# Three of four RNN heads on channel tiles in place, low halves and a channel sum by DMA, and one more conv pair in the second part

## The chip, the cores and the metric

The kernel runs on one core of a Trainium2 chip. The engines named here are PE (matrix products), ACT (functions of one tensor), DVE (elementwise work on two tensors, and scans), POOL (here it issues DMAs that add to their destination) and SP (here it only issues DMAs). The metric is the device time of one execution in microseconds; lower is better. Three runs of the kernel before took 1533.87 to 1534.23 us, median 1534.11 us.

## The reference, cut to what matters

One layer over 1024 positions and 1024 channels: a norm, two parallel branches, a gated sum and a projection, then an MLP and a final norm.

```python
h = rms_norm(x, g_mix)
z = h @ w_in + b_in                       # 7168 columns
va, ga, xb, gb, sa, sb = split(z, (1024, 1024, 1536, 1536, 1024, 1024))

u = va * sigmoid(ga)                      # conv branch
u = causal_depthwise_conv(u, conv_a_w, conv_a_b)      # 31 taps
u = silu(layer_norm(u, ln_g, ln_b))       # mean over the 1024 channels
y_a = u @ w_a_out

v = causal_depthwise_conv(xb, conv_b_w, conv_b_b)     # RNN branch, 4 taps
r = sigmoid(block_diag(v, w_rg_a) + b_rg_a)           # 16 heads of 96 channels
i = sigmoid(block_diag(v, w_rg_x) + b_rg_x)
log_a = -8 * r * softplus(-lam)
a, mult = exp(log_a), sqrt(-expm1(2 * log_a))         # mult is 1 at position 0
v = scan(h[t] = a[t] * h[t-1] + mult[t] * i[t] * v[t])
y_b = (v * gelu(gb)) @ w_b_out

x = x + (sigmoid(sa) * y_a + sigmoid(sb) * y_b) @ w_o
x = x + square(relu(rms_norm(x, g_mlp) @ w_1)) @ w_2
return rms_norm(x, g_final)
```

## The kernel before

Tensors lie with channels on the 128 partitions and the 1024 positions along the free axis. Every fp32 operand of a product is split in a high and a low half, and a product is three matmuls (high by high, low by high, high by low). A low half is made in one of two ways: ACT copies the high half and DVE subtracts it from the source, or `split_dma` lets ACT write a negated high half, ACT write the high half, and a DMA of POOL's queue add the source (L65 to L67).

**The first part.** The loop `for s in range(3, NC1)` runs over column tiles of w_in, 128 columns each; CH lists them and s is called a slot. A column tile is 48 matmuls (`chunk_mm`, L726). In a slot PE does 36 of them, then possibly the second gate product of the head that began in the slot before (`head_mm(before, 1)`), then 12 more, then possibly the first gate product of a new head (`head_mm(new, 0)`). Tiles va and ga make one tile of u (`u_out`), and each u goes through the 31-tap convolution `conv`, whose taps (L637) DVE does one by one wherever it would have nothing else to do. Tiles xb make one tile of v by ACT and three DVE taps (`xb_out`), and `xb_parts` splits v.

**The heads.** 1536 RNN channels are 12 tiles of 128 channels or 16 heads of 96, so a group g of four heads covers three tiles (3g to 3g+2). PE needs the 96 channels of a head on partitions 0 to 95, so `head_load` gathers both halves of v by DMA as PIECES says, and `head_gate` makes a head's gate in a tile of its own and scatters it by DMA to the gate tiles, which lie as v does. All gate products go through one PSUM buffer, "ps2", so a product begins only when ACT has read the one before. HS0 says in which slot each head starts: heads 0 to 3 in slots 5 to 8, heads 4 to 7 in slots 10 to 13 and so on. EXP is the slot after a group's last head: there `scan_exp` does exp and tanh of three tiles on ACT, and `scan_in` multiplies gate by v on DVE for tiles 3g and 3g+1 (3g+2 a slot later); `scan_root` follows a slot later, and `scan_tile` does the recurrence.

**The order of the work.** The order of the instructions on every engine is written by this code: `manual_schedule` keeps program order, on DMA queues too. A planner with three clocks (P, A, V for PE, ACT, DVE) adds up estimated costs; `later` notes DVE work with the time at which it is due, and `vector_work` and `fill` put conv taps ahead of it until that time. The clocks only choose the order. On the chip, an engine stands at the first instruction whose operand is not there.

**The second part.** The remaining columns (gb, sa, sb) run as pairs of column tiles in ZPAIRS. A pair is seven products of 12 matmuls each (`z_mm`, L914), a Strassen form, over sums of weight blocks (`z_sums`) split into tiles zo (`z_lhs`) and over sums of x blocks (`x_load`, `x_sum`, `x_parts`, made at the end of the first part as XS says). Then follow the product of the RNN branch, the layer norm, which begins from ysum (the sum over the conv's tiles), and the rest.

Of the kernel before, what the change touches and what calls it, by code (L numbers as in the profile page):

```python
# [9 lines left out]
F32 = mybir.dt.float32  # L10
# [5 lines left out]
P = 128  # L16
# [14 lines left out]
def trunk_kernel(ctx: ExitStack, tc: tile.TileContext, x, xt_in, xt_eo, vecs, w_in, w_a_out, w_b_pl, w_b_sq,  # L31
# [303 lines left out]
    with tc.manual_schedule(engines={mybir.EngineType.Activation, mybir.EngineType.DVE,  # L335
# [4 lines left out]

        spare = PS("spare")

# [121 lines left out]


    PIECES = [[(0, 0, 96, 0)], [(0, 96, 128, 0), (1, 0, 64, 32)],
              [(1, 64, 128, 0), (2, 0, 32, 64)], [(2, 32, 128, 0)]]

# [59 lines left out]
    def head_mm(n, gi):  # L528
        vh, vl = parts[n]
        gh, gl = gws[n]  # L530
        gps[n, gi] = ps = PS(f"rg{n}_{gi}", "ps2")
        for hf, hs in enumerate(HALVES):
            o = ps[:HD, hs]
            nc.tensor.matmul(o, gh[:, gi, :], vh[:, hs], start=True, stop=False)  # L534
            nc.tensor.matmul(o, gl[:, gi, :], vh[:, hs], start=False, stop=False)
            nc.tensor.matmul(o, gh[:, gi, :], vl[:, hs], start=False, stop=True)  # L536
        at("P", 6 * MM)

    def head_gate(n, gi, ready):
        g, hh = divmod(n, 4)  # L540
        a = H(f"g{n}_{gi}", "g")
        nc.scalar.activation(a, gps.pop((n, gi))[:HD, :], AF.Sigmoid,  # L542
                             bias=(ba_c, bx_c)[gi][:, n:n + 1])
        at("A", 1.11, ready)
        for (ti, p0, p1, d0) in PIECES[hh]:
            t = 3 * g + ti
            if (gi, t) not in gate:
                gate[gi, t] = T(f"g{gi}_{t}")
            nc.sync.dma_start(gate[gi, t][p0:p1, :], a[d0:d0 + p1 - p0, :])

# [33 lines left out]

    def u_out(j, psv, psg):

        u = T(f"u{j}")
        uv = u.rearrange("p (o n) -> p o n", o=2)
        nc.scalar.activation(uv, psg.rearrange("p (n o) -> p o n", o=2), AF.Sigmoid,
                             bias=bin_c[:, GA + j:GA + j + 1])  # L590
        later(at("A", 1.11), 1.28, nc.vector.scalar_tensor_tensor, uv,
              psv.rearrange("p (n o) -> p o n", o=2), bin_c[:, VA + j:VA + j + 1], uv,
              ALU.add, ALU.mult)
        ut[j] = u
        fresh.append(j)

    NE = WA // 2 + 1  # L600

    def conv(j):
# [42 lines left out]
        nc.sync.dma_start(yd[j], acc)  # L645
        yield step()
        if j == 0:
            ysum.append(T("ysum"))
            nc.vector.tensor_copy(ysum[0], acc)
        else:  # L650
            nc.vector.tensor_tensor(ysum[0], ysum[0], acc, add)
        yield step(1.22)

# [82 lines left out]
    def z_load(i, kk):  # L736

        zraw[i, kk] = raw = qp.tile([P, 2, 4, P], F32, tag="p", name=f"zw{i}_{kk}", bufs=4)
        c = ZPAIRS[i]
        nc.sync.dma_start(raw, w_in[c:c + 2, :, 4 * kk:4 * kk + 4, :].rearrange("m p k c -> p m k c"))  # L740

# [46 lines left out]
    def z_get(n, f):  # L788
# [15 lines left out]
    with tc.manual_schedule(engines=ENGINES):  # L804
        for s in range(3, NC1):
            w_load(s + 2)
            taps["hold"] = s > NC1 - 4
            begun = clk["P"]
# [25 lines left out]
            elif c >= GA:  # L834
                u_out(c - GA, zps[s - 2], zps[s - 1])
            w_parts(s + 1)
# [37 lines left out]
            vector_work(clk["P"] - 0.7)  # L874
            if nxt is not None:
                head_load(nxt)

# [28 lines left out]
    def z_mm(i, p):  # L906
# [10 lines left out]
        at("P", 12 * MM)  # L917

    def z_out(i, m_, hf, src, name):
        ci = ZPAIRS[i] + m_  # L920
        bias = bin_c[:, ci:ci + 1]
# [21 lines left out]
    def z_h(i, m_, hf):  # L943
        t = ZPAIRS[i] + m_ - GB
        if t < 12:
            hb[t, hf] = h = EV(f"hb{t}_{hf}")
# [33 lines left out]
    with tc.manual_schedule(engines=ENGINES):  # L980
# [155 lines left out]
        z_get(3, z_lhs)  # L1136
        u_out(7, zps[NC1 - 2], zps[NC1 - 1])
        vector_work(clk["V"])
# [1013 lines left out]
def layout(i):  # L2152
# [13 lines left out]
    def tiles(w, n=1):  # L2166
# [6 lines left out]
    mix = np.arange(D).reshape(2, 4, 4, 32).transpose(0, 2, 1, 3).ravel()  # L2173
    vecs = [cols(i[n][0]) for n in ("g_mix", "b_in")] + [cols(i["g_mlp"][0][mix])]
    vecs += [cols(i[n][0]) for n in ("conv_a_b", "ln_g", "ln_b")]
    vecs += [cols(i["conv_a_w"][0]), cols(i["conv_b_w"][0]), cols(i["conv_b_b"][0])]
    vecs += [cols(i["lam"][0])] + [heads(i[n][0]) for n in ("b_rg_a", "b_rg_x")]
    wb = i["w_b_out"][0].reshape(12, P, 8, P)
    w2 = i["w_2"][0].reshape(DFF // 512, 2, 2, P, 2, HS).transpose(0, 2, 4, 3, 1, 5)
# [45 lines left out]
```

## Time and profile before

| | |
|---|---|
| median of three runs | 1534.11 us |
| profiled execution | 1534.4 us |
| its span | 1532.6 us |
| granted PE clock, mean | 0.999 |
| first part, column tiles from 43.02 to 361.10 us | 25 slots |
| one column tile, 48 matmuls | 10.88 us |
| one Strassen product, 12 matmuls | 2.72 us |
| PE busy | 1522.9 us, 99% |
| DVE busy | 1217.2 us, 79% |
| ACT busy | 911.8 us, 59% |
| POOL busy | 172.6 us, 11% |

A row of a timeline is: start in us, duration, engine, line, operation, output and inputs by their names in the program without numbers, shape, and in brackets how long the engine idled before it and what ended that. A row of the waits names who waited, for what, how long in total, how often and the longest. Rows of DMAs name the queue (SPq, POOLq) and end with the size and the median time from issue to landing, or give the shortest, median and longest. Engines overlap, so busy shares do not sum to the span.

### The profile page before, as it was taken

Reading aid. Unit: us, or ns where it says so; the run is one execution under the profiler, and the core shown is the slowest. Engines: PE = TensorE matmul, PEld = TensorE weight load, DVE = VectorE, ACT = ScalarE, POOL = GpSimd, SP = SyncE. Lnnn points to the kernel's source line nnn. Section 1 sums busy time; section 2 is a strip of 40 time slices with the busy share of each in tenths; the row PEclk is TensorE's granted clock in tenths of the full one; section 3 lists DMA queues with packets and bytes.
Section 4 is the critical chain, followed back from the end, with each engine's and each line's share of the span. In section 5 each row is a group of like instructions: output and inputs, shape, how many; then the busy total and the mean of one; then the engine's idle time right before and its main releaser. Section 6 shows DMA issues by size and latency. Waiting matters only on the chain.

```text
span 1532.6 us, 19039 instructions
## 1 busy us (share of the span) xinstructions
PE 1522.9 (99%) x6734; PEld 1252.9 (82%) x6734; DVE 1217.2 (79%) x1647; ACT 911.8 (59%) x1273; POOL 172.6 (11%) x205
## 2 busy tenths in 40 slices
PE   9999999999999999999999999999999999999998
PEld 7878887888888888888888888888888888888886
DVE  6899999979999998778769879755555386777777
ACT  6648576657667666735475877554444455545475
POOL 0000000002222222000022322000000000101010
PEclk9999999999999999999999999999999999999999
DMA  8776978899998888963779898333333974776465
GB/s 349 198 188 159 250 185 215 223 274 224 241 255 209 198 193 229 311 230 117 265 199 301 197 194 210 138 117 112 112 112 110 304 266 124 177 209 170 109 123 153
DMA packets 132577, 304.68 MB, mean 199 GB/s; under 512 B 13264, under 2 KB 35280, under 8 KB 132480
## 3 DMA queue, kind: packets, MB, share of 16 engines
q1 hardware_dynamic: 104048, 234.79, 46.6%
q0 software_dynamic: 28288, 68.40, 24.4%
q8 instruction: 53, 0.87, 0.2%
q14 instruction: 44, 0.36, 0.1%
q10 hardware_dynamic: 144, 0.26, 0.0%
HBM read 149.79 MB, written 60.82 MB: 137 GB/s over the span
## 4 chain that ended last, share of the span: by engine, by line
PE 91%; issue 4%; DMA 2%; POOL 1%; DVE 1%; ACT 0%; SPq 0%; POOLq 0%; DVEq 0%
PE z L726 18%; PE d1b L1952 2%; PE d2b L1952 2%; PE d0b L1952 2%; PE d3b L1952 2%; PE d0e L1952 1%; PE d3e L1952 1%; PE d3a L1952 1%; PE d2e L1952 1%; PE d2a L1952 1%; PE d1e L1952 1%; PE d1a L1952 1%; PE z L258 1%; PE rg L534 1%; PE rg L536 1%
## 5 line engine op out<-in xcount | busy, mean ns | idle before, releaser
L726 PE MATMUL z<-xh,win_h 128*128 128x512 f32 x400 | 124.9, 390 | 0.0
L726 PE MATMUL z<-xl,win_h 128*128 128x512 f32 x400 | 124.5, 389 | 0.0
L726 PE MATMUL z<-xh,win_l 128*128 128x512 f32 x400 | 98.2, 391 | 0.0
L726 PEld LDWEIGHTS z<-xh,win_l 128*128 128x128 f32 x400 | 75.1, 188 | 16.9
L726 PEld LDWEIGHTS z<-xh,win_h 128*128 128x128 f32 x400 | 75.0, 188 | 16.7 <-ACT win_h L67 0.7
L637 DVE SCALAR_TENSOR_TENSOR y<-u,vec,y 128x511 f32<-128x511 f32 (+14 forms) x120 | 88.6, 739 | 0.0
L726 PEld LDWEIGHTS z<-xl,win_h 128*128 128x128 f32 x400 | 75.1, 188 | 15.8
L542 ACT ACTIVATE g<-rg,vec 96x1024 f32<-96x1024 f32 x32 | 35.6, 1113 | 85.4 <-issue 43.2
L637 DVE SCALAR_TENSOR_TENSOR yt<-u,vec,yt 128x511 f32<-128x511 f32 (+6 forms) x112 | 82.9, 740 | 0.0
L637 DVE SCALAR_TENSOR_TENSOR y<-yt,csum,y 128x511 f32<-128x511 f32 (+6 forms) x112 | 82.8, 739 | 0.0
L1648 ACT ACTIVATE o<-s 128x512 fp32r<-128x512 f32 x56 | 33.7, 623 | 45.7 <-DVE s L1632 26.4
L66 POOL DMA_DIRECT2D win_l<-win_raw x25 | 21.8, 871 | 325.0 <-ACT win_l L65 287.5
L486 DVE SCALAR_TENSOR_TENSOR v<-xb,vec,v 128x1023 f32<-128x1023 f32 (+2 forms) x36 | 46.2, 1283 | 6.9 <-ACT v L477 6.1
L66 POOL DMA_DIRECT2D zo<-zw x42 | 36.7, 874 | 127.7 <-ACT zo L65 114.6
L66 POOL DMA_DIRECT2D db_10l<-br x4 | 3.5, 874 | 339.3 <-DMA br<-in_w_dram 253.8
L1176 DVE TENSOR_TENSOR o<-s,o 128x512 fp32r<-128x512 f32 x56 | 37.3, 684 | 1.5 <-ACT o L1648 1.5
L65 ACT ACTIVATE zo<-zw 128x512 fp32r<-128x512 f32 x42 | 26.3, 625 | 20.1 <-PE z10f L914 2.1
L66 POOL DMA_DIRECT2D zo<-zs x28 | 24.5, 875 | 76.7 <-ACT zo L65 71.4
L578 DVE TENSOR_TENSOR_SCAN g<-a,g 128x1024 f32<-128x1024 f32 x12 | 27.5, 2292 | 0.4
L67 ACT ACTIVATE win_h<-win_raw 128x1024 fp32r<-128x1024 f32 x25 | 26.1, 1046 | 0.0
L65 ACT ACTIVATE win_l<-win_raw 128x1024 fp32r<-128x1024 f32 x25 | 26.1, 1045 | 0.0
L67 ACT ACTIVATE zo<-zw 128x512 fp32r<-128x512 f32 x42 | 26.1, 621 | 0.0
(3140 smaller groups left out, 4832.2 us busy)
## 6 DMA issues: line engine op xcount, KB each, us to landing
w_raw<-in_w_dram SPq DMA_DIRECT2D x34, 512.0 KB, 5.6
br<-in_w_dram SPq DMA_DIRECT2D x32, 512.0 KB, 5.9
ar<-fd SPq DMA_DIRECT2D x32, 512.0 KB, 6.8
zw<-in_w_in_dram SPq DMA_DIRECT2D x28, 512.0 KB, 5.7
win_raw<-in_w_in_dram SPq DMA_DIRECT2D x25, 512.0 KB, 7.4
win_l<-win_raw POOLq DMA_DIRECT2D x25, 512.0 KB, 7.3
zo<-zw POOLq DMA_DIRECT2D x42, 256.0 KB, 5.7
gates<-zg SPq DMA_DIRECT2D x32, 256.0 KB, 3.9
```

The costliest lines, as they stand in the source:

```text
L65: nc.scalar.activation(l, src, AF.Copy, scale=-1.0)
L66: nc.gpsimd.dma_start(l, src, accum_op=ALU.add)
L67: nc.scalar.activation(h, src, AF.Copy)
L258: nc.tensor.matmul(z0[i][:, HALVES[hf]], w0[i][w][:, k, :], xpart(a, hf, k), start=k == 0 and which == "hh", stop=k == 7 and which == ("hl ...
L486: nc.vector.scalar_tensor_tensor(v[:, d:S], a[:, 0:S - d], cbw_c[:, w * 12 + t:w * 12 + t + 1], v[:, d:S], ALU.mult, ALU.add)
L542: nc.scalar.activation(a, gps.pop((n, gi))[:HD, :], AF.Sigmoid, bias=(ba_c, bx_c)[gi][:, n:n + 1])
L578: nc.vector.tensor_tensor_scan(i, a, i, 0.0, ALU.mult, ALU.add)
L637: nc.vector.scalar_tensor_tensor(o[:, k:], a[:, 0:HS - k], c, o[:, k:], ALU.mult, add)
L726: nc.tensor.matmul(zps[s][:, HALVES[hf]], w[:, k, :], xw[k][part][hf], start=n == 0, stop=n == 23)
L1176: tt(l, src, h.bitcast(F32), ALU.subtract)
L1648: nc.scalar.activation(o[:, 0], src, AF.Copy)
L1952: nc.tensor.matmul(o, a, b, start=start and n == 0, stop=stop and n == len(todo) - 1, skip_group_check=not start or not stop)
```

## The change

- The RNN channels are permuted when the weights are laid out (`rnn`), so that three of a group's four heads lie on partitions 0 to 95 of the group's three tiles, and the fourth on partitions 96 to 127 of all three. The first three are used in place, and their gates are written straight to rows 0 to 95 of the gate tiles. Only the fourth is gathered (32 rows from each of three tiles) and its gates scattered (32 rows to each).
- `head_load` runs at a slot's start for each new tile of v, not at a slot's end for each head. HS0 begins one slot earlier (heads 0 to 3 in slots 4 to 7); EXP is still the slot after the group's last head.
- v's low halves come from `split_dma`, where DVE subtracted.
- ysum is added up by DMAs of POOL's queue, where DVE added.
- The column tiles va7 and ga7 become pair 6 of the second part (15 pairs, was 14); the first part has 23 slots, was 25. `z_u` makes the two halves of u7. The last two column tiles of the first part change places, so ACT's gate of u6 comes in the last slot and DVE's product after it.
- XS is counted from NC1. The PSUM buffer of the first warm-up products and the count in `fill` (48, now 47) change.

```diff
-            taps["now"], taps["next"], taps["left"] = taps["next"], None, 48
+            taps["now"], taps["next"], taps["left"] = taps["next"], None, 47
...
 def xb_parts(t):
     vp_[t] = T(f"vth{t}", F32R), T(f"vtl{t}", F32R)
-    nc.scalar.activation(vp_[t][0], vt[t], AF.Copy)
-    h = vp_[t][0].bitcast(F32)
-    later(at("A", 1.06), 1.22, nc.vector.tensor_tensor, vp_[t][1], vt[t], h, ALU.subtract)
+    split_dma(vt[t], *vp_[t])
+    at("A", 2.1)
...
-def head_load(n):
-    g, hh = divmod(n, 4)
-    parts[n] = H(f"vh{n}", "p", F32R), H(f"vl{n}", "p", F32R)
-    for (ti, p0, p1, d0) in PIECES[hh]:
-        for a, b in zip(parts[n], vp_[3 * g + ti]):
-            nc.sync.dma_start(a[d0:d0 + p1 - p0, :].bitcast(F32), b[p0:p1, :].bitcast(F32))
+def head_load(t):
+    n = 4 * (t // 3) + 3
+    if t % 3 == 0:
+        parts[n] = H(f"vh{n}", "p", F32R), H(f"vl{n}", "p", F32R)
+    for a, b in zip(parts[n], vp_[t]):
+        nc.sync.dma_start(a[32 * (t % 3):32 * (t % 3) + 32, :].bitcast(F32), b[HD:P, :].bitcast(F32))
+    parts[n - 3 + t % 3] = vp_.pop(t)
...
 def head_gate(n, gi, ready):
     g, hh = divmod(n, 4)
-    a = H(f"g{n}_{gi}", "g")
+    if hh < 3:
+        gate[gi, 3 * g + hh] = T(f"g{gi}_{3 * g + hh}")
+    a = gate[gi, 3 * g + hh][:HD] if hh < 3 else H(f"g{n}_{gi}", "g")
     nc.scalar.activation(a, gps.pop((n, gi))[:HD, :], AF.Sigmoid,
                          bias=(ba_c, bx_c)[gi][:, n:n + 1])
     at("A", 1.11, ready)
-    for (ti, p0, p1, d0) in PIECES[hh]:
-        t = 3 * g + ti
-        if (gi, t) not in gate:
-            gate[gi, t] = T(f"g{gi}_{t}")
-        nc.sync.dma_start(gate[gi, t][p0:p1, :], a[d0:d0 + p1 - p0, :])
+    if hh == 3:
+        for i in range(3):
+            nc.sync.dma_start(gate[gi, 3 * g + i][HD:P, :], a[32 * i:32 * i + 32, :])
...
         if j == 0:
             ysum.append(T("ysum"))
-            nc.vector.tensor_copy(ysum[0], acc)
+            nc.gpsimd.dma_start(ysum[0], acc)
         else:
-            nc.vector.tensor_tensor(ysum[0], ysum[0], acc, add)
+            nc.gpsimd.dma_start(ysum[0], acc, accum_op=add)
...
+del CH[26:]
+NU = 7
+CH[-2:] = CH[:-3:-1]
 NC1 = len(CH)
...
-ZPAIRS = [GB + 2 * i for i in range(6)] + [SA + 2 * i for i in range(4)]
+ZPAIRS = [GB + 2 * i for i in range(6)] + [VA + 7] + [SA + 2 * i for i in range(4)]
...
-HS0 = [5 + 5 * (n // 4) + n % 4 for n in range(NH)]
+HS0 = [4 + 5 * (n // 4) + n % 4 for n in range(NH)]
...
-XS = {23: ((x_load, 0),), 24: ((x_sum, 0),), 25: ((x_load, 1), (x_parts, 0, 6)),
-      26: ((x_sum, 1), (x_parts, 0, 7, 5)), 27: ((x_parts, 0, 4), (x_parts, 1, 6))}
+XS = {NC1 - 5: ((x_load, 0),), NC1 - 4: ((x_sum, 0),), NC1 - 3: ((x_load, 1), (x_parts, 0, 6)),
+      NC1 - 2: ((x_sum, 1), (x_parts, 0, 7, 5)), NC1 - 1: ((x_parts, 0, 4), (x_parts, 1, 6))}
+head_w(0)
...
         w_load(s + 2)
+        for t in sorted(vp_):
+            head_load(t)
...
         elif c >= GA:
-            u_out(c - GA, zps[s - 2], zps[s - 1])
+            if CH[s] == c - GA + VA:
+                u_gate(c - GA, zps[s - 1])
+            else:
+                u_out(c - GA, zps[s - 2], zps[s - 1])
...
-        if nxt is not None:
-            head_load(nxt)
...
+uz = {}
+def z_u(i, j, m_, hf, src):
+    if m_ and hf:
+        return
+    if (m_, hf) == (0, 0):
+        uz[j] = T(f"u{j}")
+    d = halved(uz[j], hf)
+    if m_ == 0:
+        nc.scalar.activation(d, src.rearrange("p (n o) -> p o n", o=2), AF.Sigmoid,
+                             bias=bin_c[:, GA + j:GA + j + 1])
+        ready = at("A", 0.62)
+        if hf == 0:
+            return
+        src = zb[i, "c"]
+    else:
+        ready = 0
+    later(ready, 0.74, nc.vector.scalar_tensor_tensor, d,
+          src.rearrange("p (n o) -> p o n", o=2), bin_c[:, VA + j:VA + j + 1], d,
+          ALU.add, ALU.mult)
+    if hf:
+        ut[j] = uz.pop(j)
+        fresh.append(j)
+
 def z_out(i, m_, hf, src, name):
+    if ZPAIRS[i] < GA:
+        z_u(i, ZPAIRS[i] - VA, m_, hf, src)
+        return
...
-    u_out(7, zps[NC1 - 2], zps[NC1 - 1])
+    u_mul(NU - 1, zps[NC1 - 1])
...
+r = np.arange(NH * HD).reshape(NH // 4, 4, HD)
+rnn = np.concatenate([r[:, :3], r[:, 3].reshape(NH // 4, 3, 32)], 2).ravel()
+z = np.arange(7168)
+for o in (2048, 3584):
+    z[o:o + NH * HD] = o + rnn
...
-    "w_in": tiles(i["w_in"][0]),
+    "w_in": tiles(i["w_in"][0][:, z]),
```

More of the change, by code (lines that the diff above doesn't have):

```diff
@@ L339, in trunk_kernel @@
         nc.scalar.activation(warm[:, 0:1], warm[:, 1:2], AF.Sqrt)
-        spare = PS("spare")
+        spare = PS("spare", "ps2")
         def idle_mm(n):
@@ L463, in dve @@
         return at("V", cost, ready)
-    PIECES = [[(0, 0, 96, 0)], [(0, 96, 128, 0), (1, 0, 64, 32)],
-              [(1, 64, 128, 0), (2, 0, 32, 64)], [(2, 32, 128, 0)]]
     vt = {}
@@ L528, in head_mm @@
     def head_mm(n, gi):
-        vh, vl = parts[n]
+        vh, vl = (a[:HD] for a in (parts.pop(n) if gi else parts[n]))
         gh, gl = gws[n]
@@ L583, in trunk_kernel, with u_gate, u_mul @@
     ysum = []
-    def u_out(j, psv, psg):
[L587 to L595, printed above, removed]
+    def u_gate(j, ps):
+        ut[j] = u = T(f"u{j}")
+        nc.scalar.activation(u.rearrange("p (o n) -> p o n", o=2), ps.rearrange("p (n o) -> p o n", o=2),
+                             AF.Sigmoid, bias=bin_c[:, GA + j:GA + j + 1])
+        return at("A", 1.11)
+    def u_mul(j, ps, ready=0):
+        uv = ut[j].rearrange("p (o n) -> p o n", o=2)
+        later(ready, 1.28, nc.vector.scalar_tensor_tensor, uv, ps.rearrange("p (n o) -> p o n", o=2),
+              bin_c[:, VA + j:VA + j + 1], uv, ALU.add, ALU.mult)
+        fresh.append(j)
+    def u_out(j, psv, psg):
+        u_mul(j, psv, u_gate(j, psg))
     NE = WA // 2 + 1
@@ L645, in conv @@
         nc.sync.dma_start(yd[j], acc)
-        yield step()
         if j == 0:
             ysum.append(T("ysum"))
-            nc.vector.tensor_copy(ysum[0], acc)
+            nc.gpsimd.dma_start(ysum[0], acc)
         else:
-            nc.vector.tensor_tensor(ysum[0], ysum[0], acc, add)
-        yield step(1.22)
+            nc.gpsimd.dma_start(ysum[0], acc, accum_op=add)
+        yield step()
     xbh = {1: xh[0][0:2], 2: xh[0][2:4], 3: xh[1][2:4]}
@@ L739, in z_load @@
         c = ZPAIRS[i]
+        if c < GA:
+            for m_, col in enumerate((GA + c, VA + c)):
+                nc.sync.dma_start(raw[:, m_], w_in[col, :, 4 * kk:4 * kk + 4, :])
+            return
         nc.sync.dma_start(raw, w_in[c:c + 2, :, 4 * kk:4 * kk + 4, :].rearrange("m p k c -> p m k c"))
@@ L917, in z_mm @@
         at("P", 12 * MM)
+    uz = {}
[19 more added lines that the diff above has]
+            ut[j] = uz.pop(j)
+            fresh.append(j)
     def z_out(i, m_, hf, src, name):
+        if ZPAIRS[i] < GA:
+            z_u(i, ZPAIRS[i] - VA, m_, hf, src)
+            return
         ci = ZPAIRS[i] + m_
@@ L944, in z_h @@
         t = ZPAIRS[i] + m_ - GB
-        if t < 12:
+        if 0 <= t < 12:
             hb[t, hf] = h = EV(f"hb{t}_{hf}")
@@ L2173, in layout @@
     mix = np.arange(D).reshape(2, 4, 4, 32).transpose(0, 2, 1, 3).ravel()
-    vecs = [cols(i[n][0]) for n in ("g_mix", "b_in")] + [cols(i["g_mlp"][0][mix])]
+    r = np.arange(NH * HD).reshape(NH // 4, 4, HD)
[3 more added lines that the diff above has]
+        z[o:o + NH * HD] = o + rnn
+    vecs = [cols(i["g_mix"][0]), cols(i["b_in"][0][z])] + [cols(i["g_mlp"][0][mix])]
     vecs += [cols(i[n][0]) for n in ("conv_a_b", "ln_g", "ln_b")]
-    vecs += [cols(i["conv_a_w"][0]), cols(i["conv_b_w"][0]), cols(i["conv_b_b"][0])]
-    vecs += [cols(i["lam"][0])] + [heads(i[n][0]) for n in ("b_rg_a", "b_rg_x")]
-    wb = i["w_b_out"][0].reshape(12, P, 8, P)
+    vecs += [cols(i["conv_a_w"][0]), cols(i["conv_b_w"][0][:, rnn]), cols(i["conv_b_b"][0][rnn])]
+    vecs += [cols(i["lam"][0][rnn])] + [heads(i[n][0]) for n in ("b_rg_a", "b_rg_x")]
+    wb = i["w_b_out"][0][rnn].reshape(12, P, 8, P)
     w2 = i["w_2"][0].reshape(DFF // 512, 2, 2, P, 2, HS).transpose(0, 2, 4, 3, 1, 5)
```

## The prediction

> **What bounds the kernel now.** I read the page of the profile first, then what PE waits for, then the first part's stretches, then the single rows of ACT, DVE and PE there.
>
> ```profile
> span 1532.6 us, 19039 instructions
> PE 1522.9 (99%) x6734; PEld 1252.9 (82%) x6734; DVE 1217.2 (79%) x1647; ACT 911.8 (59%) x1273; POOL 172.6 (11%) x205
> q0 software_dynamic: 28288, 68.40, 24.4%
> q1 hardware_dynamic: 104048, 234.79, 46.6%
> ```
> ```profile
> PE spare L345 <- POOL ones L113: 1.6, 1, 1.6
> PE f1d L1660 <- DMA o<-s: 0.4, 1, 0.4
> PE d0b L1952 <- DVE da_61l L1176: 0.3, 1, 0.3
> ```
> ```profile
> sum 100.00, PE 100.00 PEld 79.96 DVE 96.22 ACT 59.34 POOL 6.72; mean PE 20.00 PEld 15.99 DVE 19.24 ACT 11.87 POOL 1.34
> ```
>
> PE is the bound: busy 99% of the span, and the second fence, the whole list of PE's waits, sums to 2.3 us. The third fence is the sum of five stretches of 20 us from 80 to 180 us, in the middle of the first part: PE has no gap and DVE has under 4 us in a hundred. So work saved on DVE, ACT or a queue buys nothing by itself; only fewer matmuls do. And a delay of DVE is not caught up soon. The profiled execution took 1534.4 us, 0.3 us above the median 1534.11; sums start from 1534.4.
>
> **The matmuls.** The pair that moves costs 96 matmuls as two column tiles and 84 in the seven products of the second part.
>
> ```profile
> 43.02 10.88 PE z L726 x48
> 361.10 2.72 PE z0a L914 x12
> ```
>
> Both rows (chain of waits: start, us, work) give 0.2267 us a matmul, so 12 fewer are 2.72 us: 1534.4 - 2.7 = 1531.7. That is the whole gain that PE can show.
>
> **DMA and DVE work.** Removed: three quarters of what the head loads and gate scatters moved. Each was 16 heads x 2 x 96 rows x 4 KB = 12.6 MB, together 18.9 MB less; by the q1 row (234.79 MB for 46.6% of the span) that is 57 us of the sixteen engines. Added on POOL's queue: 12 low halves and 8 sums of 0.52 MB; by the q0 row (68.40 MB for 24.4%) 2.87 us each, 57 us. A draw: I count nothing. What hides it is that no transfer of the first part ends last for PE; without that cover one late transfer costs up to 2.87 us. On DVE 12 subtractions and 8 sums go, some 24 us:
>
> ```profile
> L462 DVE TENSOR_TENSOR vtl<-v,vth x12: 1198/1220/1226, 56.3 to 280.0; 128x1024 fp32r<-128x1024 f32 x12
> L651 DVE TENSOR_TENSOR ysum<-ysum,y x7: 1218/1224/1228, 185.0 to 602.7; 128x1024 f32<-128x1024 f32 x7
> L1193 ACT ACTIVATE mu1h<-ysum x1: 612/612/612, 643.2 to 643.2; 128x512 fp32r<-128x512 f32 x1
> ```
>
> The order written for DVE fills this with taps, so it gives no slack to what follows. The last sum, at 602.7 us, is 40 us ahead of its reader at 643.2; a DMA there is hidden. Three sums come ahead of a second-part zo load in POOL's queue: 0 to 3 x 2.87 us; I take 0, because the zo loads are issued several products ahead.
>
> **The head sequence.** Here the change adds a wait. Before, tiles 3g and 3g+1 were complete with head 4g+2. After, all three gate tiles take 32 rows of head 4g+3. Yet scan_in of tiles 3g and 3g+1 (DVE's product of gate and v) is still issued in the slot of the exponentials, the very slot in which ACT makes head 4g+3's second gate. In DVE's new order these products stand right behind v3's three taps, with fifteen conv taps and v4 queued behind them. ACT's splitting of v4 waits for v4, the next gates stand behind that split, and PE's next head waits for the gates, since all heads share the PSUM buffer ps2. The rows for this, from before (timelines of ACT, DVE, SP's queue and PE):
>
> ```profile
> 107.08 1.25 ACT L477 ACTIVATE v<-xb,vec 128x1024 f32<-128x1024 f32 x1
> 115.37 1.10 ACT L542 ACTIVATE g<-rg,vec 96x1024 f32<-96x1024 f32 x1
> 130.32 0.35 ACT L522 ACTIVATE rgh<-rraw 96x192 fp32r<-96x192 f32 x1
> 130.68 1.28 ACT L558 ACT_TABLE_LOAD   x1
> 138.68 1.10 ACT L474 ACTIVATE xb<-z,vec 128x1024 f32<-128x1024 f32 x1
> 139.81 1.24 ACT L477 ACTIVATE v<-xb,vec 128x1024 f32<-128x1024 f32 x1
> 140.96 1.04 ACT L65 ACTIVATE win_l<-win_raw 128x1024 fp32r<-128x1024 f32 x1
> 141.91 1.04 ACT L67 ACTIVATE win_h<-win_raw 128x1024 fp32r<-128x1024 f32 x1
> ```
> ```profile
> 110.40 3.91 DVE L486 SCALAR_TENSOR_TENSOR v<-xb,vec,v 128x1023 f32<-128x1023 f32 x3
> 128.19 2.35 DVE L462 TENSOR_TENSOR g<-g,v 128x1024 f32<-128x1024 f32 x2
> 131.87 0.74 DVE L637 SCALAR_TENSOR_TENSOR yt<-u,vec,yt 128x508 f32<-128x508 f32 x1
> 140.39 0.74 DVE L637 SCALAR_TENSOR_TENSOR y<-u,vec,y 128x503 f32<-128x503 f32 x1
> ```
> ```profile
> 116.49 1.12 SPq L549 DMA_DIRECT2D g<-g  x2
> DMA to landing us min/median/max: 2.4/4.2/14.3
> g<-g SPq DMA_DIRECT2D x16, 128.0 KB, 5.1
> ```
> ```profile
> 104.85 8.18 PE z L726 x36
> 114.03 0.40 PE L536 MATMUL rg<-vl,rgh 96*96 96x512 f32 x1
> 118.19 0.39 PE L536 MATMUL rg<-vl,rgh 96*96 96x512 f32 x1
> ```
>
> Durations: a split of v by two ACT passes 1.9 (the two win rows start 0.95 apart); gate 1.1; exp group 8.0 (130.68 to 138.68); xb with its v pass 2.3; w_parts 2.0; v's three taps 3.9; fourteen taps from 131.87 to the v taps that follow 140.39, 0.66 each; two products 2.3. A slot is 10.88 us and 1.39 for each head product (six matmuls) in it. PE stands at a slot's first head after 8.2 us (104.85, 36 matmuls), at its second after 8.2 + 1.39 + 2.72 = 12.3.
>
> Group 0, times from the start of slot 8. ACT's v pass ends at 3.5 (108.33 - 104.85), the v3 taps at 7.7. Two splitting passes to 9.65, gate(3,1) to 10.75. Its 32 rows are issued at once (116.49 stands right behind 115.37 + 1.10) and land 4.2 later, at 15.0. The wait is bounded by 2.4 and by 14.3 us of landing, the ends of that view; I take the median, near the 5.1 of pieces of this size. So DVE, which had no gap there, stands from 7.7 to 15.0: 7.3 us. Then two products to 17.3, fifteen taps and a weight subtraction (10.1) to 27.4, v4 to 31.3. Slots 8 and 9 hold one head product each, 12.27 us long, so slot 10 begins at 24.5 and v4 is ready at 6.8 of slot 10. ACT: two splits, weight split 0.35, table 1.28, gate(4,0) 1.1: done at 11.5, where PE has wanted it since 8.2. **PE stalls 3.3.** DVE goes on with one product (1.2), eleven taps and a weight subtraction (7.5), v5: 19.4. ACT: two splits and gate(4,1), 22.4. PE's second head of slot 10 is now due at 11.5 + 1.39 + 2.72 = 15.6. **PE stalls another 6.8.** Sum 10.1 us.
>
> Groups 1 and 2 have the same order behind their products (fifteen taps, v, one product, eleven taps, v; slots 15 and 20), and in between DVE comes back to its plan, because the planner's clock does not pass PE's and PE has been held back too. So 3 x 10.1 = 30 us.
>
> **The end of the first part.** The last group's gate moves one column tile (10.9 us) closer to the end of the first part. Behind it on ACT come the exponentials, roots, halves of the x sums and then the first zo tiles:
>
> ```profile
> 325.78 1.12 ACT L542 ACTIVATE g<-rg,vec 96x1024 f32<-96x1024 f32 x1 [5.57 <-issue]
> 344.50 1.28 ACT L589 ACT_TABLE_LOAD   x1 [2.37 <-DVE g L577]
> 352.17 1.06 ACT L67 ACTIVATE xs5h<-xs 128x1024 fp32r<-128x1024 f32 x1 [1.46 <-DMA yd<-y]
> 353.14 0.61 ACT L65 ACTIVATE zo<-zw 128x512 fp32r<-128x512 f32 x1
> 354.04 0.87 POOL L66 DMA_DIRECT2D zo<-zw  x1 [2.17 <-ACT zo L65]
> zo<-zw POOLq DMA_DIRECT2D x42, 256.0 KB, 5.7
> ```
>
> The first zo lands at 354.0 + 5.7 = 359.7, and PE uses its low half from about 361.4: 1.7 to spare. ACT idles 2.4 + 1.5 in the chain. 10.9 - 1.7 - 3.9 = 5.3 remain; the chain loses one w_parts (2.0) and gains one u gate with its table (2.4): 5 to 7 us without any delay on DVE. DVE is blocked here too (g9 waits for head 15): xs6's high half waits for taps behind the products, u5 for its low half, and the last w_parts behind u5 end at 28.8 of slot 23, where PE is done with the tile before at 23.2: 5.6; root (4.2), three halves (3.1), u6's table and gate (2.4) and zo (0.6, POOL 0.9, landing 5.7) make 45, due at 40: 5 more. With the next zo I take 11.
>
> **Sum:** 1534.4 - 2.7 + 30 + 11 = 1572.7; forecast 1572.
>
> The Trainium skill ("DMA: Bandwidth & Descriptors", section on the anatomy of one DMA) gives a DMA a fixed cost of about 2.0 us plus its bytes at 436 GB/s. For the 128 KB piece that is, as an estimate from that page, 2.3 us; the block would be 5.4 us and the sum about 1565. The trace's fastest landing, 2.4, agrees with it, but the median of 4.2 beside other traffic does not, and I go by the median.
>
> **Rivals.**
> A, not slower: ACT and DVE are far enough ahead that gate and v products are ready when PE asks. For it: before, PE never waits in this part, though the gate at 115.37 ends only 0.7 us before PE's next head (117.2, 1.39 before 118.58) takes its buffer. The point that decides is v5: its taps must end by 9.2 of slot 10, since 1.9 of splits and 1.1 of gate must end by 12.3. Against it: the v pass on ACT alone stands behind the exp group and ends past that. Time: 1531.7, within 0.2% of before, faster by a hair more if the start gains too. 0.2% (3.1 us) is about what a measurement of this kernel can tell from no change.
> B, the products don't block: the piece lands before DVE arrives, since DVE is itself late. Then only the order on ACT is left (the split of v5 ahead of gate(4,1)): v4 at -0.5 of slot 10, root and splits to 5.1, gate(4,0) 7.9, xb5 10.2, v5 14.1, gate(4,1) 17.1, where 12.3 was due: 4.8 a group, with 6.7 at the end. 1531.7 + 14.4 + 6.7 = 1553.
> C, the block is larger: landings of 5.1 and more behind other transfers, POOL's v low halves late for their heads (issue 0.9, landing 5.7 and more). Each group 13 and the end 14: 1531.7 + 39 + 14 = 1585.
>
> **How the numbers follow.** Forecast 0.50, B 0.24, C 0.16, A 0.10. A lies on both sides of the bound: faster 0.04, same 0.05, the rest to slower. The range drops A and the outer half of C: from B's 1553 less its own doubt of 5, to 1586. The slower cases alone hold 0.91.
>
> **What would show it.** In the changed kernel PE should wait for ACT's gates (rg behind g) two times in slots 10, 15 and 20, some 10 us each; DVE should idle about 7 us ahead of the products g<-g,v with a DMA of g as releaser, four times; PE should wait for the last win_h and for zo at the end of the first part; the rest, from the second pair on, should run as before. No DVE idle at the products means B; no PE wait at all in the first part means A. A second part that is longer than 15 pairs of 19.05 us (7 x 2.72) would show that the sums delay zo, which I counted at nothing.

## The result and the profile after

The changed kernel takes 1584.47 us (median of four runs, 1583.08 to 1587.39) and the kernel before 1534.17 us (four runs). The ratio is 1.0329, 95% interval 1.0312 to 1.0347: the change makes the kernel slower by 50 us. The forecast was 1572 us, slower, with a range of 1548 to 1586. The profiled execution took 1583.1 us.

The page of the changed kernel (first two lines) and the list of what PE waits for, which answer to the first two fences of the prediction:

```profile
span 1581.3 us, 18971 instructions
PE 1536.4 (97%) x6722; PEld 1259.9 (80%) x6722; DVE 1199.5 (76%) x1636; ACT 929.4 (59%) x1299; POOL 192.3 (12%) x228
```
```profile
PE rg L531 <- ACT g L541: 25.6, 6, 5.2
PE z0a L921 <- DMA zo<-zw: 4.5, 2, 3.8
PE z L725 <- ACT win_h L67: 4.5, 1, 4.5
PE spare L345 <- POOL ones L113: 1.6, 1, 1.6
```

PE waited 2.3 us in all before. Now it waits six times for a gate, and at the end of the first part once for win_h and twice for zo: 34.6 us that were not there. PE's busy time should have fallen by 2.7 us to 1520.2 and rose to 1536.4 instead: 16.2 us more for fewer matmuls. Together these are 50.8 us; less the 2.7 us of matmuls, 48.1 of the 48.7 us by which the span grew.

Where the 16.2 us are shows in stretches of 20 us around the first group (columns: stretch, its length, busy time of PE, PEld, DVE, ACT and POOL with the number of instructions, granted PE clock, DMA share, GB/s), and in the first matmul of each of four head products there:

```profile
120.00:140.00 20.00, 20.00 (x90) 16.36 (x89) 16.77 (x22) 16.50 (x16) 0.86 (x1) 1.00 0.61 136
140.00:160.00 20.00, 12.51 (x37) 8.86 (x36) 19.66 (x25) 14.61 (x16) 3.36 (x4) 0.74 0.61 130
160.00:180.00 20.00, 20.00 (x89) 16.12 (x88) 13.68 (x16) 5.37 (x6) 0.95 (x2) 1.00 0.62 166
```
```profile
131.04 0.40 PE L531 MATMUL rg<-vth,rgh 96*96 96x512 f32 x1
...
144.31 0.74 PE L531 MATMUL rg<-vth,rgh 96*96 96x512 f32 x1 [3.53 <-ACT g L541]
...
155.06 0.47 PE L531 MATMUL rg<-vth,rgh 96*96 96x512 f32 x1 [3.96 <-ACT g L541]
...
166.33 0.40 PE L531 MATMUL rg<-vth,rgh 96*96 96x512 f32 x1
```

Between these rows lie 42, 18 and 42 matmuls, at 0.2267 us 9.52, 4.08 and 9.52 us. They took 13.27, 10.75 and 11.27: lost are 3.75, 6.67 and 1.75 us. Of the 6.67 only 3.96 is a wait. In the rest PE works, but slowly: the granted clock is 0.74 in the mean of that stretch. The first group loses 12.2 us. By the same count the second loses 4.59 + 6.68 + 1.73 = 13.0 us and the third 5.42 + 6.69 + 1.70 = 13.8 us (first and last row of each):

```profile
208.84 0.40 PE L531 MATMUL rg<-vth,rgh 96*96 96x512 f32 x1
...
244.96 0.40 PE L531 MATMUL rg<-vth,rgh 96*96 96x512 f32 x1
```
```profile
287.47 0.40 PE L531 MATMUL rg<-vth,rgh 96*96 96x512 f32 x1
...
324.40 0.40 PE L531 MATMUL rg<-vth,rgh 96*96 96x512 f32 x1
```

The three groups cost 39.0 us. What holds up DVE, ACT and PE there is in the timelines of DVE and ACT:

```profile
112.42 3.92 DVE L483 SCALAR_TENSOR_TENSOR v<-xb,vec,v 128x1023 f32<-128x1023 f32 x3
123.16 2.36 DVE L462 TENSOR_TENSOR g<-g,v 128x1024 f32<-128x1024 f32 x2 [6.83 <-DMA g<-g]
135.57 3.91 DVE L483 SCALAR_TENSOR_TENSOR v<-xb,vec,v 128x1023 f32<-128x1023 f32 x3
147.99 3.92 DVE L483 SCALAR_TENSOR_TENSOR v<-xb,vec,v 128x1023 f32<-128x1023 f32 x3
```
```profile
118.34 1.10 ACT L541 ACTIVATE g<-rg,vec 96x1024 f32<-96x1024 f32 x1
139.57 1.06 ACT L65 ACTIVATE vtl<-v 128x1024 fp32r<-128x1024 f32 x1 [3.32 <-issue]
143.14 1.11 ACT L541 ACTIVATE g<-rg,vec 96x1024 f32<-96x1024 f32 x1
152.00 1.06 ACT L65 ACTIVATE vtl<-v 128x1024 fp32r<-128x1024 f32 x1 [3.58 <-DVE v L483]
153.91 1.09 ACT L541 ACTIVATE g<-rg,vec 96x1024 f32<-96x1024 f32 x1
```

DVE ends v3 at 116.3 and stands until the 32 rows of gate(3,1) (ACT, 118.34) have landed. Then come the products, the taps, and only at 135.57 v4. ACT splits v4 at 139.57 and makes gate(4,0) at 143.14; PE goes on at 144.31. The same again for v5, its split and gate(4,1). This is the chain that the prediction walked through, link for link.

How long DVE stands differs: 6.83, 8.62 and 9.63 us in the three groups. The 32 rows land later from group to group (shortest, median and longest time from issue to landing of the three pieces of each):

```profile
DMA to landing us min/median/max: 3.0/3.7/3.8
DMA to landing us min/median/max: 4.4/5.1/5.1
DMA to landing us min/median/max: 5.2/5.9/6.1
```

For the last group and the end of the first part, one row of each kernel tells how far behind PE is at the last head's second product:

```profile
324.14 0.40 PE L534 MATMUL rg<-vh,rgh 96*96 96x512 f32 x1
```
```profile
351.86 0.40 PE L531 MATMUL rg<-vh,rgh 96*96 96x512 f32 x1
```

In the changed kernel this product comes one column tile earlier, so 351.86 - (324.14 - 10.88) = 38.6 us have been lost up to there. The span lost 48.7 + 2.7 = 51.4 us in all, so 12.8 us came later. They lie at the end of the first part; after that the second part runs as forecast. There DVE stands at the last group's products, ACT's gate of u5 then waits for xs6's low half behind them, and PE for the weights that ACT splits after that gate:

```profile
356.88 2.36 DVE L462 TENSOR_TENSOR g<-g,v 128x1024 f32<-128x1024 f32 x2 [11.44 <-issue]
367.25 1.28 ACT L584 ACT_TABLE_LOAD   x1 [3.01 <-DVE xs6l L462]
371.60 1.22 PE L725 MATMUL z<-xh,win_h 128*128 128x512 f32 x2 [4.53 <-ACT win_h L67]
```

### The profile page after: what moved, and what is told of

It reads as the page before. It is cut to its first block, busy times and chain, and to the rows that moved or that the text cites. A ratio compares the mean times of both kernels' runs of the same rounds, so it can differ in the third digit from the quotient of the medians.

```text
span 1581.3 us, 18971 instructions
## 1 busy us (share of the span) xinstructions
PE 1536.4 (97%) x6722; PEld 1259.9 (80%) x6722; DVE 1199.5 (76%) x1636; ACT 929.4 (59%) x1299; POOL 192.3 (12%) x228
## 4 chain that ended last, share of the span: by engine, by line
PE 76%; DVE 10%; issue 7%; DMA 4%; ACT 1%; POOL 1%; SPq 0%; POOLq 0%; ACTq 0%; DVEq 0%
PE z L725 5%; DVE y L634 3%; DVE v L483 2%; PE d2b L1987 2%; PE d1b L1987 2%; PE d0b L1987 2%; DVE yt L634 2%; PE d3b L1987 2%; PE d0e L1987 1%; PE d3e L1987 1%; PE d3a L1987 1%; PE d2e L1987 1%; PE d2a L1987 1%; PE d1e L1987 1%; PE d1a L1987 1%
## 5 line engine op out<-in xcount | busy, mean ns | idle before, releaser
L725 PE MATMUL z<-xh,win_h 128*128 128x512 f32 x368 | 118.3, 400 | 4.6 <-ACT win_h L67 4.5
L725 PE MATMUL z<-xl,win_h 128*128 128x512 f32 x368 | 116.9, 396 | 0.0
L725 PE MATMUL z<-xh,win_l 128*128 128x512 f32 x368 | 93.6, 400 | 0.0
L725 PEld LDWEIGHTS z<-xh,win_h 128*128 128x128 f32 x368 | 70.9, 193 | 21.0 <-ACT win_h L67 5.4
L725 PEld LDWEIGHTS z<-xl,win_h 128*128 128x128 f32 x368 | 71.1, 193 | 15.4
L1683 ACT ACTIVATE o<-s 128x512 fp32r<-128x512 f32 x56 | 33.7, 623 | 45.7 <-DVE s L1667 26.4
L531 PE MATMUL rg<-vth,rgh 96*96 96x512 f32 x48 | 21.3, 444 | 25.6 <-ACT g L541 25.6
L65 ACT ACTIVATE zo<-zw 128x512 fp32r<-128x512 f32 x45 | 28.2, 627 | 24.0 <-PE z1f L921 2.1
L462 DVE TENSOR_TENSOR g<-g,v 128x1024 f32<-128x1024 f32 x12 | 14.3, 1222 | 36.5 <-DMA g<-g 25.1
L65 ACT ACTIVATE vtl<-v 128x1024 fp32r<-128x1024 f32 x12 | 12.7, 1059 | 38.2 <-DVE v L483 31.0
L531 PEld LDWEIGHTS rg<-vth,rgh 96*96 96x96 f32 x48 | 8.4, 175 | 31.1 <-ACT g L541 28.5
```

Source lines behind the costliest of these rows:

```text
L65: nc.scalar.activation(l, src, AF.Copy, scale=-1.0)
L462: f(*a)
L725: nc.tensor.matmul(zps[s][:, HALVES[hf]], w[:, k, :], xw[k][part][hf], start=n == 0, stop=n == 23)
L1683: nc.scalar.activation(o[:, 0], src, AF.Copy)
```

## The experiments

"Up to the last head" below is the loss against the kernel before at that product; "the end" is what the span of the profiled execution loses beside it (with 2.7 us added where the pair is moved). All comparisons are with the kernel before on the same chip.

### e1: the products later

```diff
-                        scan_in(begun + 3.5, 3 * g, 3 * g + 1)
+                        scan_in(begun + 15.5, 3 * g, 3 * g + 1)
```

> The changed kernel with one edit: the products of gate and v for tiles 3g and 3g+1 stand ten conv taps later on DVE (due 15.5 us after the slot's start instead of 3.5). Theory W (DVE blocked by these products delays v4, and with it ACT's gates and PE; a PE that has waited 3.5 us or more then runs at half the granted clock for some us): DVE's idle time ahead of the products falls from 36.5 us to under 6, the first PE wait of each group (3.5, 4.4, 5.2 us) nearly goes, the second (4.0, 4.0, 4.5) stays at 4 to 5 because the split of v5 still stands ahead of the gate on ACT; the end of the first part loses about 6 instead of 10. Sum: about 1562 us (1555 to 1568). Rival O (only the order on ACT matters, DVE's idle time does not): 1580 or more. Rival S (the low halves and sums on POOL's queue cost the time): no change, 1584.

Measured: 1566.61 us (1.0210, 1.0194 to 1.0225). PE's first wait of each group is gone, the second stays:

```profile
PE rg L531 <- ACT g L541: 14.0, 3, 5.0
```

Taking DVE's blocked time away was worth 18 us. The place is right, and the time is within the range given for theory W; O and S fall. The end did not get cheaper as expected: 12.0 us, where some 6 in place of 10 were expected. DVE still idles 7.4 us ahead of the products, where the expectation had under 6, and 5.7 of them are put down to a DMA of the channel sum.

### e2: the gate ahead of the split

```diff
                 vector_work(0)
+                if before is not None:
+                    head_gate(before, 1, clk["P"] - 12 * MM)
                 xb_parts(0 if s == 3 else c - XB)
-            if before is not None:
+            elif before is not None:
                 head_gate(before, 1, clk["P"] - 12 * MM)
```

> The changed kernel with one edit: in slots that split a tile of v, ACT makes the second gate of the head before ahead of the split and not behind it. Theory W: the first wait of each group stays, the second goes, with its share of slow clock: about 1566 us (1560 to 1573). Rival (DVE alone is the cause and the order on ACT adds nothing): 1580 or more.

Measured: 1561.85 us (1.0182, 1.0166 to 1.0197). The waits for gates fall from 25.6 to 9.7 us. Changing the order on ACT alone is worth 23 us, as expected, and more than freeing DVE. The two gains overlap: together (e3) they are 30 us, not 41.

### e3: both

> The changed kernel with both edits, the later products and the gate ahead of the split. Theory W: the waits of PE on gates fall to 0 to 2 us a group, too short to lower the clock; what stays is the end of the first part (win_h and zo, 6 to 8 us with slow clock): about 1543 us (1537 to 1549). If the waits had another cause (landings of low halves, PSUM buffer alone), over 1555.

Measured: 1554.07 us (1.0128, 1.0113 to 1.0143).

```profile
PE z0a L923 <- DMA zo<-zw: 6.1, 2, 3.8
PE z L725 <- ACT win_h L67: 4.0, 4, 2.2
PE rg L531 <- ACT g L541: 3.6, 6, 0.8
```

The gate waits fall to 0.4 and 0.8 us each, and the clock stays at 1.00 through them. The loss up to the last head is 7.3 us, of 38.6: the two causes together carry four fifths of it. The time is above the range given, because the end did not become cheaper: 15.0 us.

### e4: PE kept busy in its waits

```diff
+                if s in (10, 15, 20):
+                    zps[s] = PS(f"z{s}")
+                    for _ in range(33):
+                        nc.tensor.matmul(zps[s][:, HALVES[0]], wst[s][0][:, 0, :], xw[0][0][0],
+                                         start=True, stop=True)
                 chunk_mm(s, 0, 18)
```

> The changed kernel with 33 more matmuls (7.5 us, their result is thrown away) at the start of slots 10, 15 and 20, in a buffer that the slot's own column tile then overwrites. They fill the time in which PE waited, so PE does not idle there. Theory W: the waits of 25.6 us become busy time of about the same length, the granted clock stays at 1.00 in these slots, and the 12 to 13 us of PE busy time that slow clock adds there go: about 1572 us (1568 to 1576). Rival (the matmuls are slow after a wait for another reason, such as contention for data): 1584 or more; if the waits were not fixed in time by ACT and DVE, the 22.5 us of added matmuls come on top: 1600.

Measured: 1584.70 us (1.0323, 1.0306 to 1.0341), no change; a miss. The first wait was filled, and the clock was 1.00 until the second. Yet ACT made gate(4,1) at the same time, here:

```profile
153.72 1.09 ACT L541 ACTIVATE g<-rg,vec 96x1024 f32<-96x1024 f32 x1
```

It was 153.91 without the filling. PE waited 2.63 us there and went on at 154.87, instead of 155.06. So the slow clock between the first and the second wait costs nothing by itself: PE would have waited for the same gate. Only slow clock behind the last wait of a chain is lost, and there was at least as much of it here: 3.1, 1.7 and 3.0 us in the three groups, where the changed kernel has 1.7 in each (this stretch lies behind that second wait; the columns are as above):

```profile
156.00:158.00 2.00, 2.00 (x7) 1.38 (x6) 1.95 (x3) 0.22 (x1) 0.00 (x0) 0.50 0.85 221
```

By the medians the 22.5 us of added matmuls cost nothing either (the profiled execution was the slowest of the four and lost 3.6 us more than the changed kernel's up to the last head). The time of a group is that of the chain on DVE and ACT.

### e5 and e12: the DMAs alone, in the kernel before

e5 makes v's low halves and the channel sum by DMA in the kernel before, e12 the low halves alone.

```diff
-        nc.scalar.activation(vp_[t][0], vt[t], AF.Copy)
-        h = vp_[t][0].bitcast(F32)
-        later(at("A", 1.06), 1.22, nc.vector.tensor_tensor, vp_[t][1], vt[t], h, ALU.subtract)
+        split_dma(vt[t], *vp_[t])
+        at("A", 2.1)
...
-            nc.vector.tensor_tensor(ysum[0], ysum[0], acc, add)
-        yield step(1.22)
+            nc.gpsimd.dma_start(ysum[0], acc, accum_op=add)
+        yield step()
```

> The kernel before with two parts of the change alone: v's low halves by the POOL queue's DMA (12 times), where DVE subtracted, and the channel sum by DMA (8 times). Heads, slots and pairs as before. Theory: the work these take off DVE buys nothing and the DMAs are hidden, so PE keeps going: 1534 us (1532 to 1538). Rival S (the DMAs of POOL's queue are late for their heads or for the column tiles behind them): 2 to 3 us for each group and more, 1540 to 1550.

> The kernel before with v's low halves alone by DMA, the channel sum on DVE again. Tells which of the two parts of e5_before_dma_lows (1555 us) costs. The waits of PE for vl in its first two groups and the 10 us that its groups lose belong to the low halves, the 13 us at the end may belong to either: about 1546 us (1540 to 1556). If the sums cost all: 1534 to 1538.

Measured: e5 1554.96 us (1.0133, 1.0118 to 1.0148), a miss; e12 1544.72 us (1.0072, 1.0054 to 1.0090), as expected. In the kernel before, these DMAs are not free. Up to the last head e5 loses 9.2 us and e12 2.7, at the end 13.5 and 6.9. So the channel sums by DMA, which e5 has beside the low halves, add 10.2 us to the low halves' 10.6. In e5 PE waits for a gathered low half, and an ACT gate waits for its tile, which the DMA before it has not yet emptied; both DMAs stand in SP's queue:

```profile
119.65 0.47 PE L535 MATMUL rg<-vl,rgh 96*96 96x512 f32 x1 [1.68 <-DMA vl<-vtl]
```
```profile
125.80 1.11 ACT L541 ACTIVATE g<-rg,vec 96x1024 f32<-96x1024 f32 x1 [9.49 <-DMA g<-g]
```

Both landed late: the low half 10.6 us after its issue, the scatter, issued at 113.22, 12.47 us after. The low half was also issued late, at 109.03 in place of 103.82, because SP's queue first stood 4.6 us at the store of a conv tile (yd, issued at 107.96). From 112 to 124 us the DMA engines are busy without a gap in e5 (share 1.02 to 1.05), where the kernel before shows 0.92, 0.62 and 0.69. The scattered pieces between 100 and 128 us land in 3.2 us in the kernel before, 7.2 in e12 (where the same gate waits 4.33 us) and 10.1 in e5:

```profile
g<-g SPq DMA_DIRECT2D x3, 128.0 KB, 3.2
g<-g SPq DMA_DIRECT2D x3, 128.0 KB, 7.2
g<-g SPq DMA_DIRECT2D x3, 128.0 KB, 10.1
```

At the end of e12 the longest wait of ACT is for the scan of DVE:

```profile
354.37 1.28 ACT L588 ACT_TABLE_LOAD   x1 [9.52 <-DVE g L577]
```

DVE has no gap before it: the time that the subtractions left was filled with taps that now stand ahead of that scan. Gathered heads have no part in this. PE then waits 5.76 us for the last win_h behind it.

### e6: the roots later

e3 with the square roots of the first three groups a slot later:

```diff
-            if s - 1 in EXP:
-                scan_root(EXP[s - 1])
+            if EXP.get(s - 1) == 3:
+                scan_root(3)
...
+            if EXP.get(s - 2, 3) < 3:
+                scan_root(EXP[s - 2])
             if nxt is not None:
```

> e3_both and one more edit: for the first three groups the square roots (a table load and three passes, 4.2 us of ACT) come a slot later, behind the second gate. Theory F (what PE still loses there, 2.75 us a group, is that ACT has no time left from the exponentials to that gate): the loss falls to under 0.8 a group, with one more table load where ACT has time: about 1548 us (1546 to 1551). Rival (what is left is DVE's late v): 1553 or more.

Measured: 1551.51 us (1.0109, 1.0094 to 1.0124), just above the range. Up to the last head 3.1 us are lost in place of 7.3, about 1 us a group, and no wait of PE for a gate is left in the list. That ACT was out of time is right for the groups. The end took back part of it (15.8 us).

### e7 and e8: zo first

At the end of the first part: the last w_parts ahead of u5, zo(0,1) and zo(1,1) ahead of the roots, zo(0,2) and zo(1,2) ahead of the last x halves. e7 is e3 with that, e8 is e6 with that.

```diff
...
+            if s == NC1 - 2:
+                w_parts(s + 1)
             if c >= XB:
...
-            w_parts(s + 1)
+            if s == NC1 - 2:
+                z_get(0, z_lhs)
+                z_get(1, z_lhs)
+            else:
+                w_parts(s + 1)
...
         z_get(3, z_lhs)
+        x_parts(1, 6)
+        x_parts(0, 4)
         u_mul(NU - 1, zps[NC1 - 1])
```

> e3_both and one more edit, at the end of the first part alone: the last column tile's weights are split ahead of u5, the first two zo tiles ahead of the roots, the next two ahead of the last x halves. Theory: the end of the first part costs e3 about 13 us (2.3 wait for win_h, 2.6 and 3.8 for zo, the rest slow clock after these waits); the first two waits go, the third shrinks: about 1546 us (1543 to 1550). Rival (the transfers of zo are late for the traffic they meet, not for their order): 1553 or more.

> All edits: later products, gate first, later roots, zo first. The gains should add: about 1540 us (1536 to 1545). The changed kernel with nothing lost would take 1531.7 (before less 12 matmuls). If the gains do not add, 1546 or more.

Measured: 1551.91 us (1.0114, 1.0097 to 1.0131) and 1549.96 us (1.0100, 1.0085 to 1.0116). Both are misses: the gain at the end is 3.2 us in e7 and 1.9 in e8. The waits for zo's DMAs of the first pairs went, and another took their place, in e7:

```profile
PE z0a L926 <- ACT z0b L992: 6.9, 1, 6.9
```

### e9 and e10: the pair back in the first part

e9 is the changed kernel, e10 is e6, each with va7 and ga7 in the first part again.

```diff
-    del CH[26:]
-    NU = 7
-    CH[-2:] = CH[:-3:-1]
...
-    ZPAIRS = [GB + 2 * i for i in range(6)] + [VA + 7] + [SA + 2 * i for i in range(4)]
+    ZPAIRS = [GB + 2 * i for i in range(6)] + [SA + 2 * i for i in range(4)]
...
-        u_mul(NU - 1, zps[NC1 - 1])
+        u_out(7, zps[NC1 - 2], zps[NC1 - 1])
```

> The changed kernel with its last part undone: the column tiles va7 and ga7 stay in the first part (25 slots, 14 pairs), so the last group's exponentials are three tiles further from the end; 12 matmuls more (2.7 us). Theory: what the end of the first part costs the changed kernel (about 12.5 us with slow clock) comes from that closeness and goes; the 39 us of the three groups stay: about 1575 us (1571 to 1579). Rival (the end costs as much wherever it is, from the new DMAs of POOL's queue, as the kernel before with these DMAs alone lost 13 us there): 1584 to 1588.

> e6_root_later with the pair back in the first part. Theory: its groups lose 1.5 us each and its end some 15; with the end far away about 1540 us (1536 to 1544). Rival as for e9_pair_back: 1551 to 1555.

Measured: e9 1583.99 us (1.0322, 1.0303 to 1.0340) and e10 1548.26 us (1.0092, 1.0076 to 1.0108). Both miss. With two more column tiles between the last group and the end (the expectation says three, but 23 slots become 25), the end still costs 11.0 and 10.7 us. But the waits are others: at the end PE waits 1.3 us for win_h, where it waited 4.5, and no longer for zo. Instead it waits for DVE's product of u7. In e9:

```profile
PE z0b L907 <- DVE u L462: 6.5, 1, 6.5
```

In e10, where this wait is 6.7 us, the trace leads further back. DVE's product of u7 stands behind a low half of xs6, for which DVE idles; ACT makes the high half only after two waits for weight loads of the second part (zw), the longer one here:

```profile
368.32 1.23 DVE L462 TENSOR_TENSOR xs6l<-xs,xs6h 128x1024 fp32r<-128x1024 f32 x1 [7.67 <-ACT xs6h L679]
364.29 0.63 ACT L65 ACTIVATE zo<-zw 128x512 fp32r<-128x512 f32 x1 [6.64 <-DMA zw<-in_w_in_dram]
```

SP's queue issued these loads from 344.95 us on, behind the store of a scan at 340.41 that it had not had to pass before: in the kernel before they went out from 337.25 us on, ahead of that store (346.78). They landed in 15.4 us (median), where the kernel before had 8.6. So e9 and e10 exchange one loss for another of its size. The waits that the prediction gave to closeness went; whether closeness alone causes them in the changed kernel is not shown by these two runs.

### e14: e10 with the low halves by DVE

The edit is the first half of e5's diff, backwards.

> e10_root_later_pair_back with v's low halves made by DVE again (one ACT pass less and one subtraction more for each of 12 tiles, 12 DMAs less). Theory: with heads in place nothing of PE waits for the low halves, so only ACT's 0.95 us a tile counts: 0 to 3 us faster than that kernel. Rival (the DMAs of the low halves cost here as in the kernel before): 5 us and more faster.

Measured: 1549.90 us (1.0101, 1.0085 to 1.0117), 1.6 us above e10, where 0 to 3 us below were expected. Up to the last head 1.3 us are lost in place of 3.3, at the end 14.3 in place of 10.7. With heads in place the DMAs of the low halves cost nothing in sum that these two kernels show. That the 2.7 us which e12 loses up to the last head belong to the gathered heads agrees with this; its 6.9 us at the end are a matter of taps. The sums are made by DMA in both of these kernels: without them, and with the low halves by DVE while the pair is moved, nothing was tried.

| | us | up to the last head | the end |
|---|---|---|---|
| changed kernel | 1584.5 | 38.6 | 12.8 |
| e1 products later | 1566.6 | 22.1 | 12.0 |
| e2 gate first | 1561.9 | 17.5 | 12.9 |
| e3 both | 1554.1 | 7.3 | 15.0 |
| e6 roots later | 1551.5 | 3.1 | 15.8 |
| e7 zo first | 1551.9 | 7.7 | 11.8 |
| e8 all | 1550.0 | 3.3 | 13.9 |
| e9 pair back | 1584.0 | 39.7 | 11.0 |
| e10 roots later, pair back | 1548.3 | 3.3 | 10.7 |
| e14 lows by DVE | 1549.9 | 1.3 | 14.3 |
| e12 before, lows by DMA | 1544.7 | 2.7 | 6.9 |
| e5 before, lows and sums by DMA | 1555.0 | 9.2 | 13.5 |

None of these is as fast as the kernel before.

## Why the prediction was right, point by point

The measured 1584.5 us lies 12.5 us above the forecast and only 1.5 us inside the end of the range. The sum had 41 us of loss, the kernel has 52.8 (beside 1531.7). The direction and the chain are the prediction's; that the range held is in part luck, because two terms were too small in the same direction.

- **What bounds.** Right. DVE has 18 us less work and the kernel is slower; 48.1 of the 48.7 us lost are waits of PE and longer work on PE, which is slow clock where it was looked at.
- **The matmuls.** Right: the second part takes 2.72 us a product with no wait after the first pairs, and the changed kernel has 12 instructions fewer on PE (6734 to 6722).
- **DMA and DVE work at nothing.** Not refuted for the changed kernel, where neither a low half nor a sum appears in PE's list of waits. The reason given, that these DMAs are hidden, does not hold in general: in the kernel before they cost 10 and 20 us (e12, e5). Part of that goes with gathered heads, and I had treated the two as independent. But part is work taken off DVE, whose place taps take (the end of e12), and a list of PE's waits does not show such a cost by its name. For the low halves e14 finds none in sum; what the sums cost the changed kernel is open.
- **The head sequence.** The chain is right and was undone link by link: the products (e1), the split ahead of the gate (e2), both (e3), ACT's lack of time (e6). In group 0 the sizes are right as well: 3.3 and 6.8 us were forecast, 3.75 and 6.67 lost, the second as 3.96 of waiting and 2.71 of slow clock that ran while the gate was not yet made. The term that was mis-sized is the 10.1 us taken for every group; it was 13.0 on average. Part is the slow clock after the second wait (1.7 us each), which the sum did not have. Part is that the second and third group were taken for copies of the first. The 32 rows landed in 5.1 and 5.9 us there (medians), where 4.2 were taken and the first group had 3.7. So DVE idled longer, 8.6 and 9.6 us in place of 6.8, and the first loss grew to 4.6 and 5.4.
- **The end of the first part.** 11 us forecast, 12.8 measured; the waits are those named (win_h 4.5 for 5.6, zo 4.5 for 5), and the rows above show the links named for the first of them: DVE at the products, xs6's low half, u5, win_h. (The terms of the second wait add up to 45.7, not 45.) The sum had no slow clock here either. How much of it is the column tile by which the last group came closer stays open, since e9 and e10 put another loss in its place. What costs the end 11 to 16 us in every variant stays open too: each edit there moved the wait to another operand (win_h, zo, the copy z0b, u7's product), and in e5 and e12 the DMAs alone cost the end 13.5 and 6.9 us with the heads where they were. I can show that the end depends on a tight order of DVE, ACT and SP, not which order would be free.
- **The rivals.** A fell with the first wait. B fell in the profile: DVE idles 36.5 us in all ahead of the products. B's 1553 is close to e3's 1554, but e3 takes away the order on ACT too, and with the products alone unblocked (e1) it is 1567. C's time, 1585, is what was measured, and C is right in part: the pieces landed in 5.1 us and more in the second and third group, though not in the first (3.7) or the last (2.3). No head waits for a low half from POOL, the other half of C, and slow clock, which C did not have, makes up the rest; so that its number fits so closely is luck. The Trainium skill ("DMA: Bandwidth & Descriptors", section on the anatomy of one DMA), which the prediction set beside its sum, states its fit for DMAs that gpsimd issues; these pieces are issued by SP, and its 2.3 us lies below all of them but the last group's.

## What to carry to other kernels

When tiles begin to share a producer, look for every consumer that was scheduled by the old producer: here products whose gates were complete with a group's third head came to need the fourth, and kept their place in an in-order queue. A planner that does not know of a wait will put it anywhere, and the cost is not that engine's idle time but what is queued behind it. Where a chain on other engines fixes a time, filling the waiting engine with work, or speeding it up, changes nothing; only what happens behind the last wait counts (e4).

## What the runs showed that I had not expected

PE runs at half its clock after a wait of a few microseconds. A matmul that starts every 0.23 us started every 0.43 us after the wait of 3.53 us (144.84 and 145.27 are the next two starts), and the clock came back some microseconds later; in the changed kernel this makes up the 16.2 us of PE's time, though part of it lies in the shadow of the next wait (e4). The Trainium skill ("TensorE: Matmul & The Clock Gate", Part 1) says that the clock falls to half after an idle window of about 3.4 us and returns after a busy one, and that the windows run freely. The half clock agrees. The limit is softer here: in e2 a wait of 2.46 us was followed by half clock (0.50 from 146 to 148 us), and one of 2.54 us in the next group was not (1.00 from 216 to 218 us). Waits of 0.8 us in e3 left it at 1.00. Over all the traces of this case, from 40 us on, no wait of up to 1.7 us was followed by half clock, four of the nine waits between 2.2 and 2.6 us were (the shortest 2.25 us, in e3), and all 36 of 2.63 us and more were, at once or within 2 us.

```profile
146.00:148.00 2.00, 2.00 (x6) 1.60 (x5) 2.00 (x4) 2.00 (x3) 0.22 (x1) 0.50 0.44 102
```
```profile
216.00:218.00 2.00, 2.00 (x10) 1.60 (x9) 2.00 (x5) 1.97 (x3) 0.00 (x0) 1.00 0.28 62
```
